# The memory's weights split by adding DMA loads, and S5's sums moved off VectorE and GpSimd, in phase 1 of a streaming encoder step

## The chip, the cores and the metric

The kernel runs on one core of a Trainium2 chip. The time is the device time of one execution in microseconds (us); three executions of the kernel before took 1894.32, 1894.64 and 1896.23 us (median 1894.64). Engines are named as in the profile: PE (TensorE, matrix products; PEld its weight loads), DVE (VectorE), ACT (ScalarE), POOL (GpSimd) and SP (SyncE, which issues most DMAs). Each engine works through its own instructions strictly in order and waits on semaphores for the others.

## The reference, cut to what matters

One inference step of a two-layer encoder, for a prompt of 512 tokens and a running stream of 32, width 1024. Layer 0 mixes tokens with S5, a complex diagonal state-space model in 64 groups of 16 channels with 64 states each; layer 1 uses retention. Each layer then attends to 256 memory tokens and ends in a convolutional feed-forward part.

```python
def s5_discretise(a_re, a_im, log_dt, b_re, b_im, c_re, c_im):
    lam = lax.complex(a_re, a_im)
    dt = jnp.exp(log_dt)[:, None]
    a_bar = jnp.exp(lam * dt)
    b_bar = ((a_bar - 1.0) / lam)[..., None] * lax.complex(b_re, b_im)
...
def s5_block(state, u, a_bar, b_bar, c):
    bu = jnp.einsum('gpc,blgc->blgp', b_bar, u)
    bu = bu.at[:, 0].add(a_bar * state)
    _, xs = lax.associative_scan(_linear_combine, (a, bu), axis=1)
    y = jnp.real(jnp.einsum('gcp,blgp->blgc', c, xs))
...
def memory_kv(mem, g_mem, w_kv):
    m = rms_norm(mem, g_mem) @ w_kv
    k, v = jnp.split(m, 2, axis=-1)
```

All of it is float32. The memory's keys and values of both layers depend on no token, so they can be worked out at any time before the attention of their layer.

## The kernel before, in words

The program runs in stages. Phase 1 computes S5 for all tokens and, in the gaps on PE, the memory's keys and values for both layers. Behind it come the GLU of S5 (its first products are line L233), the attention of layer 0, the feed-forward part, and layer 1.

**Weights in one or two parts.** A float32 product on PE is issued in full (two instructions on PE for one product) or in parts: an operand is rounded to `hi` (type fp32r), `lo` is the rest, and three quick products hi x hi, hi x lo and lo x hi replace the full one (`mm3`, L224 to L226). `weights` loads a tile of 128 x 1024 into one of three raw slots `wr` on SP's queue (L211); `split` rounds it on ACT into one of three slots `wh` (L206) and subtracts on DVE into one of three slots `wl` (L207).

**The memory.** `kv_units` yields the work in units: for each layer an operand step (memory times gain), 8 key tiles and 8 quarters of values, each with one weight tile. `KV_SPLIT = (1,)` names the layers that are worked out in parts: layer 1. Layer 0 takes the raw weights (L492) with full float32 products (L500). The memory's 1 / rms, `mc`, needs square sums (POOL, L447), a small product (L453) and three Newton steps on DVE (`rsqrt_of`, L311 to L315); PE lays it along a row, `mr` (L340), and the keys leave PSUM times `mr` on DVE (L521).

**S5.** Discretisation comes first: `exp_acc`, an exponential by a polynomial on DVE (L620 to L630, twice), sine and cosine on ACT, powers 0 to 8 of the step (`Pr`, `Pi`, by `cmul`, L552 to L557), then `b_bar` (`bb`). The inputs `U` (8 tiles of 128 x 560) need their own 1 / rms, `ur`: ACT squares the eight tiles (L699, L702), POOL adds them up (L703), DVE reduces (L704), PE sums over partitions with the matrix `block` (L707), and DVE takes Newton steps (L709 on). `phases` builds unit phases of a chunk's step to the powers 0 to 64 by squaring (`cmul`) and renormalising (`unit`, L732 to L737), with POOL for half of the wide products. Then, for each eighth e of the groups:

- `matrices` (M): POOL multiplies U by `ur` (L781); DVE makes four products of 128 x 512 in slots of the tags `wh` and `wl` (L789, L790), POOL adds them in pairs (L791), PE turns them (L797) and multiplies with c (L802), ACT copies.
- `states` (S): PE products (L823), four DVE products with the phases (L834 to L838), two POOL sums (L836, L839), two copies (L840, L841), the scans on DVE (L847), and the way back on DVE and POOL (L849 to L860).
- `carry` (C): two DVE products for each half (L873, L875) and their sum on POOL (L877).
- `outputs` (O): PE products (L888, L889), a gelu on ACT (L890), transposes (L898), copies (L900, L901).

The source gives steps in the order of the tables PROLOGUE and ORDER, with the memory's units let in by `fill`; a scheduler then sets the order of instructions on each engine. Slots of a tag are reused in turn, and who reuses one waits until its last reader is done.

Of the kernel before, what the change touches and what calls it, by code (L numbers as in the profile page):

```python
# [13 lines left out]
OP = mybir.AluOpType  # L14
# [38 lines left out]
def constants():  # L53
    """Arrays that depend on shapes alone."""
# [27 lines left out]
def w_tiles(w, mt=None):  # L82
    """[K, M] -> [m tile, 128 of k, K/128 * 128 of m]: one contiguous chunk for an output tile."""
    k, m = w.shape
    a = w.reshape(k // P, P, m // P, P).transpose(2, 1, 0, 3)
    return a.reshape(m // P, P, (k // P) * P)


def layout(inp):
# [29 lines left out]
    cr, ci = f["ssm_c_re"][0], f["ssm_c_im"][0]      # [G, C, 64]  # L119
# [19 lines left out]
    # values: [layer, half of columns, quarter of k, 128, 2 k tiles * 512]  # L139
# [1222 lines left out]
```

## Time and profile before

| | |
|---|---|
| median of three executions | 1894.64 us |
| profiled execution, span from first to last instruction | 1893.0 us |
| PE busy over the span | 1820.2 us (96%) |
| DVE, ACT, POOL busy | 1086.7, 611.6, 384.7 us |
| DMA | 178.02 MB, mean 94 GB/s |
| mean granted PE clock | 0.980 |
| first product of the GLU | at about 248 us |

The profile gives of its own execution the span; what lies around the span is seen against the runs' median. In a row of a timeline stand start, length, engine, line and operation, output and inputs, and the number of instructions merged; in square brackets the idle time of the engine ahead of the row and what ended it. A row of waits has the sum, the number of times and the longest. A group has its count, busy time, mean length in ns, and idle time ahead of it. Where one line has several instructions that overlap, the distance from start to start is the price, not the length.

### The profile page before, as it was taken

Reading aid. Unit: us, or ns where it says so; the run is one execution under the profiler, and the core shown is the slowest. Engines: PE = TensorE matmul, PEld = TensorE weight load, DVE = VectorE, ACT = ScalarE, POOL = GpSimd, SP = SyncE. Lnnn points to the kernel's source line nnn. Section 1 sums busy time; section 2 is a strip of 40 time slices with the busy share of each in tenths; the row PEclk is TensorE's granted clock in tenths of the full one; section 3 lists DMA queues with packets and bytes.
Section 4 is the critical chain, followed back from the end, with each engine's and each line's share of the span. In section 5 each row is a group of like instructions: output and inputs, shape, how many; then the busy total and the mean of one; then the engine's idle time right before and its main releaser. Section 6 shows DMA issues by size and latency. Waiting matters only on the chain.

```text
span 1893.0 us, 32752 instructions
## 1 busy us (share of the span) xinstructions
PE 1820.2 (96%) x13785; PEld 1730.6 (91%) x13785; DVE 1086.7 (57%) x1848; ACT 611.6 (32%) x901; POOL 384.7 (20%) x439
## 2 busy tenths in 40 slices
PE   7868899999999999999999999999999999999998
PEld 6457789999999999999899899998999999999998
DVE  9999856545544535555644646546655554453553
ACT  3132454433323323333223122223444332232333
POOL 7685611011211202121000100100101121120221
PEclk9888989999999999999999999999999999999998
DMA  6434344122222222232222222222411222222221
GB/s 214 132 114 124 120 133 144 68 86 79 90 90 88 78 92 90 72 109 82 76 85 94 79 79 73 90 79 86 138 68 56 87 84 88 90 84 95 90 71 67
DMA packets 65970, 178.02 MB, mean 94 GB/s; under 512 B 8928, under 2 KB 18528, under 8 KB 65824
## 3 DMA queue, kind: packets, MB, share of 16 engines
q1 hardware_dynamic: 65536, 175.79, 27.4%
q8 instruction: 108, 1.77, 0.4%
q14 instruction: 38, 0.31, 0.1%
q10 hardware_dynamic: 288, 0.15, 0.0%
HBM read 162.78 MB, written 10.77 MB: 92 GB/s over the span
## 4 chain that ended last, share of the span: by engine, by line
PE 83%; DVE 2%; issue 1%; ACT 1%; ACTq 0%; DVEq 0%
PE ps L233 74%; PE ps L224 2%; PE ps L225 2%; PE ps L226 2%; PE ps L1286 1%; DVE wl L207 0%; PE ps L1275 0%; PE ps L1248 0%; PE ps L1008 0%; PE ps L1222 0%; ACT wh L206 0%; PE bank L1022 0%; DVE xl L292 0%; PE ps L329 0%; PE ps L403 0%
## 5 line engine op out<-in xcount | busy, mean ns | idle before, releaser
L206 ACT CAST wh<-wr 128x1024 fp32r<-128x1024 f32 (+1 forms) x256 | 264.6, 1037 | 810.2 <-PE ps L233 626.8
L233 PE MATMUL ps<-xh,wh 128*128 128x272 f32 x2432 | 507.5, 290 | 5.4 <-DVE x L356 3.6
L233 PE MATMUL ps<-xl,wh 128*128 128x272 f32 x2432 | 503.6, 288 | 0.0
L233 PE MATMUL ps<-xh,wl 128*128 128x272 f32 x2432 | 502.3, 288 | 0.0
L233 PE MATMUL ps<-r,wh 128*128 128x272 f32 x2688 | 449.2, 289 | 3.0 <-ACT r L901 1.6
L233 PEld LDWEIGHTS ps<-xh,wh 128*128 128x128 f32 x2432 | 380.7, 188 | 11.1 <-ACT r L298 3.7
L233 PEld LDWEIGHTS ps<-r,wh 128*128 128x128 f32 x2688 | 380.2, 189 | 6.4 <-ACT r L206 3.0
L233 PEld LDWEIGHTS ps<-xh,wl 128*128 128x128 f32 x2432 | 382.0, 188 | 2.3 <-issue 2.3
L233 PEld LDWEIGHTS ps<-xl,wh 128*128 128x128 f32 x2432 | 383.0, 189 | 0.3
L207 DVE TENSOR_TENSOR wl<-wr,wh 128x1024 fp32r<-128x1024 f32 (+1 forms) x256 | 321.8, 1260 | 92.3 <-ACT wh L206 84.2
L233 PE MATMUL ps<-r,wl 128*128 128x272 f32 x1344 | 278.0, 288 | 0.0
L233 PEld LDWEIGHTS ps<-r,wl 128*128 128x128 f32 x1344 | 211.2, 189 | 0.0
L356 DVE TENSOR_TENSOR x<-ps,x 128x544 f32<-128x544 f32 x96 | 69.3, 724 | 234.9 <-PE ps L233 234.7
L301 POOL TENSOR_TENSOR acc<-acc,r 128x544 f32<-128x544 f32 x36 | 58.8, 1633 | 453.1 <-ACT r L298 444.6
L1088 POOL COPY nco<-r 128x2 f32<-128x2 f32 x44 | 13.9, 315 | 374.5 <-DVE r L1086 374.5
L1095 DVE TENSOR_TENSOR r<-ps,rr 128x544 f32<-128x544 f32 x44 | 31.9, 725 | 96.7 <-PE ps L233 96.7
L1085 DVE TENSOR_TENSOR r<-ps,rr 128x272 f32<-128x272 f32 x44 | 19.4, 442 | 117.4 <-PE ps L233 117.4
L1146 POOL TENSOR_TENSOR r<-r,r 128x544 f32<-128x544 f32 x8 | 10.8, 1353 | 339.9 <-ACT wh L206 326.0
L1096 POOL TENSOR_TENSOR r<-r,r 128x32 f32<-128x32 f32 x44 | 34.3, 780 | 206.2 <-ACT wh L206 186.2
L206 ACT CAST r<-r 128x544 fp32r<-128x544 f32 x84 | 52.5, 650 | 65.8 <-POOL r L1096 26.2
L1093 DVE SCALAR_TENSOR_TENSOR r<-r,conv,r 128x546 f32<-128x546 f32 x88 | 69.1, 785 | 3.5 <-ACT r L1091 1.9
L207 DVE TENSOR_TENSOR r<-r,r 128x544 fp32r<-128x544 f32 x84 | 59.3, 729 | 14.5 <-ACT r L206 14.3
(354 smaller groups left out, 2109.0 us busy)
## 6 DMA issues: line engine op xcount, KB each, us to landing
wr<-in_w_r SPq DMA_DIRECT2D x48, 512.0 KB, 3.2
wr<-in_w_a SPq DMA_DIRECT2D x44, 512.0 KB, 3.2
wr<-in_w_g SPq DMA_DIRECT2D x44, 512.0 KB, 3.2
wr<-in_w_d SPq DMA_DIRECT2D x32, 448.0 KB, 3.2
wr<-in_w_k SPq DMA_DIRECT2D x16, 512.0 KB, 4.9
wr<-in_w_v SPq DMA_DIRECT2D x16, 512.0 KB, 3.6
wr<-in_w_q SPq DMA_DIRECT2D x16, 512.0 KB, 4.0
wr<-in_w_o SPq DMA_DIRECT2D x16, 512.0 KB, 3.3
```

The lines of the kernel that those rows point to most:

```text
L206: self.nc.scalar.copy(hi, src)
L207: (self.nc.gpsimd if pool else self.nc.vector).tensor_tensor(out=lo, in0=src, in1=hi.bitcast(F32), op=OP.subtract)
L224: mm(out, lhsT=a[0], rhs=b[0], start=start, stop=False)
L225: mm(out, lhsT=a[0], rhs=b[1], start=False, stop=False)
L226: mm(out, lhsT=a[1], rhs=b[0], start=False, stop=stop)
L233: mm(ps[:, h, :TH], lhsT=ws[wi], rhs=x[xi][:, h * TH:(h + 1) * TH], start=start and n == 0, stop=stop and n == 2)
L301: add.tensor_tensor(out=self.acc, in0=self.acc, in1=sq, op=OP.add)
L356: self.nc.vector.tensor_tensor(out=self.halves(x), in0=src, in1=self.halves(x), op=OP.add)
L1085: V.tensor_tensor(out=ext[:, 2:2 + TH], in0=pa[:, 0, :TH], in1=r[:, :TH], op=OP.mult)
L1093: V.scalar_tensor_tensor(out=cv, in0=ext[:, t:t + W], scalar=cw[:, t, f:f + 1], in1=cv, op0=OP.mult, op1=OP.add)
L1095: V.tensor_tensor(out=self.halves(gr), in0=pg[:, :, :TH], in1=self.halves(r), op=OP.mult)
L1096: PL.tensor_tensor(out=gr[:, TP:], in0=gr[:, TP:], in1=cv[:, TP + 2:W], op=OP.mult)
```

## The change

1. `KV_SPLIT = (0, 1)`: layer 0's memory products go in parts too, as layer 1's.
2. A new `weights_loaded` for all 32 tiles of the memory's weights: ACT rounds (`hi`), ACT writes `lo = -hi`, and a DMA on POOL's queue loads the same weights again and adds them to `lo`. No DVE subtraction is left there.
3. `matrices` and `carry`: POOL's sums L791 (16) and L877 (16) become adding DMAs between SBUF tiles, 8 of 128 x 1024 and 16 of 128 x 512.
4. The square sums of U: instead of POOL's seven additions and one small product, PE multiplies every squared tile with `block` in PSUM (16 products of 280 columns), and DVE reduces the result.
5. `exp_acc` joins a product and an addition to one operation; `square` and `unit` work on real and imaginary part together.

Comments are left out in the new file, so its line numbers lie 11 to 13 higher. Cut to its core:

```diff
-KV_SPLIT = (1,)          # layers whose memory projections take operands in two parts
+KV_SPLIT = (0, 1)
...
+    def weights_loaded(self, src):
+
+        raw = self.main.tile([P, 1024], F32, tag="wr", bufs=3, name=self.name("wr"))
+        self.nc.sync.dma_start(out=raw, in_=src)
+        hi = self.main.tile([P, 1024], F32R, tag="wh", bufs=3, name=self.name("wh"))
+        lo = self.main.tile([P, 1024], F32R, tag="wl", bufs=3, name=self.name("wl"))
+        self.nc.scalar.copy(hi, raw)
+        self.nc.scalar.activation(out=lo, in_=hi.bitcast(F32), func=AF.Copy, scale=-1.0)
+        self.nc.gpsimd.dma_start(out=lo, in_=src, accum_op=OP.add)
+        return hi, lo
...
             if l in KV_SPLIT:
-                return self.weights(src)
+                return self.weights_loaded(src)
...
-            V.tensor_scalar(out=p, in0=r, scalar1=1.0 / 5040, scalar2=1.0 / 720, op0=OP.mult, op1=OP.add)
-            for c in (1.0 / 120, 1.0 / 24, 1.0 / 6, 0.5, 1.0, 1.0):
-                V.tensor_tensor(out=p, in0=p, in1=r, op=OP.mult)
-                V.tensor_scalar(out=p, in0=p, scalar1=c, scalar2=None, op0=OP.add)
+            V.tensor_scalar(out=p, in0=r, scalar1=1.0 / 5040, scalar2=None, op0=OP.mult)
+            for c in (1.0 / 720, 1.0 / 120, 1.0 / 24, 1.0 / 6, 0.5, 1.0):
+                V.scalar_tensor_tensor(out=p, in0=p, scalar=c, in1=r, op0=OP.add, op1=OP.mult)
...
-        red, ssum = self.slot(SLOT), st([P, POS], "ssum")
+        ssum = st([P, POS], "ssum")
+        ps = self.bank()
         for e in range(KT):
-            if e == 0:
-                A.activation(out=red, in_=U[e], func=AF.Square)
-            else:
-                sq = self.slot(SLOT)
-                A.activation(out=sq, in_=U[e], func=AF.Square)
-                PL.tensor_tensor(out=red, in0=red, in1=sq, op=OP.add)
-        V.tensor_reduce(out=ssum, in_=red.rearrange("p (g q) -> p q g", g=8), axis=AX.X, op=OP.add)
+            sq = self.slot(SLOT)
+            A.activation(out=sq, in_=U[e], func=AF.Square)
+            for n in range(2):
+                nc.tensor.matmul(ps[:, :4 * POS], lhsT=block, rhs=sq[:, n * 4 * POS:(n + 1) * 4 * POS],
+                                 start=e == 0 and n == 0, stop=e == KT - 1 and n == 1)
+        V.tensor_reduce(out=ssum, in_=ps[:, :4 * POS].rearrange("p (g q) -> p q g", g=4), axis=AX.X, op=OP.add)
...
+        def square(o, a):
+
+            V.tensor_tensor(out=wt, in0=a, in1=a, op=OP.mult)
+            V.tensor_tensor(out=o[:, 0], in0=wt[:, 0], in1=wt[:, 1], op=OP.subtract)
+            V.scalar_tensor_tensor(out=o[:, 1], in0=a[:, 0], scalar=2.0, in1=a[:, 1], op0=OP.mult, op1=OP.mult)
...
             for n in range(2):
                 V.tensor_tensor(out=vb[n], in0=pw[n], in1=bs[n], op=OP.mult)
                 V.tensor_tensor(out=vt[n], in0=pw[2], in1=bs[1 - n], op=OP.mult)
-                PL.tensor_tensor(out=vb[n], in0=vb[n], in1=vt[n], op=OP.add)
+            nc.gpsimd.dma_start(out=vbt, in_=vtt, accum_op=OP.add)
...
-                PL.tensor_tensor(out=y, in0=y, in1=yt, op=OP.add)
+                nc.gpsimd.dma_start(out=y, in_=yt, accum_op=OP.add)
```

The scheduler also moves what stands around these edits. On PE, where the row `mr` of the memory's 1 / rms is laid (L340 before, the operand is `ident` and `mc`), the order before was, with seven key tiles of layer 0 ahead of it (the last in bank_331):

```order
L500 MATMUL bank_331<-r_105,wr_329 128x256 x2
L500 MATMUL bank_331<-r_108,wr_329 128x256 x2
L500 MATMUL bank_331<-r_111,wr_329 128x256
L340 MATMUL bank_241<-ident,mc 128x128 x2
L500 MATMUL bank_331<-r_111,wr_329 128x256
L500 MATMUL bank_346<-r_102,wr_344 128x256 x2
```

It is now, with wh and wl the two parts of a weight tile, bank_131 the first key tile, bank_257 the second and L464 the square sum for `mc`:

```order
L237 MATMUL bank_131<-r_128,wl_99 128x256
L464 MATMUL bank_282<-ones,r_156 128x1 x2
L235 MATMUL bank_307<-r_107,wh_302 128x256
L236 MATMUL bank_307<-r_107,wh_302 128x256
L235 MATMUL bank_340<-r_107,wh_335 128x256
L236 MATMUL bank_340<-r_107,wh_335 128x256
L351 MATMUL bank_282<-ident,mc 128x128 x2
L237 MATMUL bank_257<-r_107,wl_253 128x256
```

One key tile is complete ahead of L351, of three others only the first products with the rounded part stand there.

On POOL, where U is multiplied by `ur` (L781, now L791), the order before was, with the sums of three eighths' matrices (L791) far ahead and the sums of the first states behind:

```order
L791 TENSOR_TENSOR wh_528<-wh_528,wl_529 128x512 x2
L791 TENSOR_TENSOR wh_772<-wh_772,wl_773 128x512 x2
L791 TENSOR_TENSOR wh_949<-wh_949,wl_950 128x512 x2
...
L781 TENSOR_TENSOR u_158<-u_158,ur_463 128x560
...
L781 TENSOR_TENSOR u_165<-u_165,ur_463 128x560
L836 TENSOR_TENSOR r_742<-r_742,r_743 128x280
```

It is now, where L229 is the adding load of a weight tile and L802 the adding transfer of an eighth's matrices:

```order
L229 DMA wl_685<-in_w_v 128x1024
L229 DMA wl_704<-in_w_v 128x1024
L791 TENSOR_TENSOR u_191<-u_191,ur_651 128x560
...
L791 TENSOR_TENSOR u_198<-u_198,ur_651 128x560
L229 DMA wl_731<-in_w_v 128x1024
L802 DMA wh_765<-wl_766 128x1024
L802 DMA wh_967<-wl_968 128x1024
L229 DMA wl_1026<-in_w_v 128x1024
L847 TENSOR_TENSOR r_937<-r_937,r_938 128x280
```

The first two eighths' matrix sums moved from ahead of the eight products to behind them, and twelve adding loads stand ahead of them.

On DVE the Newton steps for `ur` follow the reduction of the square sums (L716); before, they were spread over the phases' operations. They stand now behind the last key tile of layer 0 (bank_497, times `mr`) and ahead of the first matrices' products:

```order
L532 TENSOR_TENSOR rr_486<-bank_461,mr 128x256
L532 TENSOR_TENSOR acc_522<-bank_497,mr 128x256
L716 TENSOR_REDUCE ssum_614<-bank_615 128x70
L719 TENSOR_SCALAR um_649<-ssum_614 128x70
L322 TENSOR_SCALAR ur_651<-um_649 128x70
...
L801 TENSOR_TENSOR wl_766<-PIn_577,bbi_603 128x512
```

The matrices' products of the first three eighths stood ahead of the reduction of the square sums before.

More of the change, by code (lines that the diff above doesn't have):

```diff
@@ L623, in exp_acc @@
             V.scalar_tensor_tensor(out=r, in0=k, scalar=2.12194440e-4, in1=r, op0=OP.mult, op1=OP.add)
-            V.tensor_scalar(out=p, in0=r, scalar1=1.0 / 5040, scalar2=1.0 / 720, op0=OP.mult, op1=OP.add)
-            for c in (1.0 / 120, 1.0 / 24, 1.0 / 6, 0.5, 1.0, 1.0):
-                V.tensor_tensor(out=p, in0=p, in1=r, op=OP.mult)
-                V.tensor_scalar(out=p, in0=p, scalar1=c, scalar2=None, op0=OP.add)
+            V.tensor_scalar(out=p, in0=r, scalar1=1.0 / 5040, scalar2=None, op0=OP.mult)
+            for c in (1.0 / 720, 1.0 / 120, 1.0 / 24, 1.0 / 6, 0.5, 1.0):
+                V.scalar_tensor_tensor(out=p, in0=p, scalar=c, in1=r, op0=OP.add, op1=OP.mult)
             ki = st([P, N], "ki", dt=I32)
             V.tensor_scalar(out=ki, in0=k, scalar1=127.0, scalar2=8388608.0, op0=OP.add, op1=OP.mult)
-            V.tensor_tensor(out=out, in0=p, in1=ki.bitcast(F32), op=OP.mult)
+            V.scalar_tensor_tensor(out=out, in0=p, scalar=1.0, in1=ki.bitcast(F32), op0=OP.add, op1=OP.mult)
         t3 = [sm(f"t{n}") for n in range(3)]
-        dt, zr, zi, rho, cs, sn = (sm(n) for n in ("dt", "zr", "zi", "rho", "cs", "sn"))
+        dt, zr, zi, rho = (sm(n) for n in ("dt", "zr", "zi", "rho"))
+        csn = st([P, 2, N], "csn")
+        cs, sn = csn[:, 0], csn[:, 1]
         exp_acc(dt, ldt, t3)
@@ L694, in phase1 @@
                   [a.rearrange("p (n c) -> p n c", c=C) for a in braw], bt)
-        red, ssum = self.slot(SLOT), st([P, POS], "ssum")
+        ssum = st([P, POS], "ssum")
+        ps = self.bank()
         for e in range(KT):
-            if e == 0:
-                A.activation(out=red, in_=U[e], func=AF.Square)
-            else:
-                sq = self.slot(SLOT)
-                A.activation(out=sq, in_=U[e], func=AF.Square)
-                PL.tensor_tensor(out=red, in0=red, in1=sq, op=OP.add)
-        V.tensor_reduce(out=ssum, in_=red.rearrange("p (g q) -> p q g", g=8), axis=AX.X, op=OP.add)
+            sq = self.slot(SLOT)
[4 more added lines that the diff above has]
+        V.tensor_reduce(out=ssum, in_=ps[:, :4 * POS].rearrange("p (g q) -> p q g", g=4), axis=AX.X, op=OP.add)
         fill(F_NORM)
-        ps = self.bank()
-        nc.tensor.matmul(ps[:, :POS], lhsT=block, rhs=ssum, start=True, stop=True)
         um, ut, ur = st([P, POS], "um"), st([P, POS], "ut"), st([P, POS], "ur")
-        V.tensor_scalar(out=um, in0=ps[:, :POS], scalar1=1.0 / D, scalar2=EPS, op0=OP.mult, op1=OP.add)
+        V.tensor_scalar(out=um, in0=ssum, scalar1=1.0 / D, scalar2=EPS, op0=OP.mult, op1=OP.add)
         self.rsqrt_of(um, ur, ut)
@@ L725, in phase1 @@
         pr, pi = ph[:, 0], ph[:, 1]
-        w1 = [st([P, NP, 1], f"w1{n}") for n in range(2)]
-        w2 = [st([P, NP, 1], f"w2{n}") for n in range(2)]
-        wt = [st([P, NP, 1], f"wt{n}") for n in range(2)]
-        def unit(c):
-            V.tensor_tensor(out=wt[0], in0=c[0], in1=c[0], op=OP.mult)
-            V.tensor_tensor(out=wt[1], in0=c[1], in1=c[1], op=OP.mult)
-            V.tensor_tensor(out=wt[0], in0=wt[0], in1=wt[1], op=OP.add)
-            V.tensor_scalar(out=wt[0], in0=wt[0], scalar1=-0.5, scalar2=1.5, op0=OP.mult, op1=OP.add)
-            for a in c:
-                V.tensor_tensor(out=a, in0=a, in1=wt[0], op=OP.mult)
+        w1, w2, wt = (st([P, 2, NP, 1], f"w{n}") for n in range(3))
+        def square(o, a):
+            V.tensor_tensor(out=wt, in0=a, in1=a, op=OP.mult)
+            V.tensor_tensor(out=o[:, 0], in0=wt[:, 0], in1=wt[:, 1], op=OP.subtract)
+            V.scalar_tensor_tensor(out=o[:, 1], in0=a[:, 0], scalar=2.0, in1=a[:, 1], op0=OP.mult, op1=OP.mult)
+        def unit(c):
+            V.tensor_tensor(out=wt, in0=c, in1=c, op=OP.mult)
+            V.tensor_tensor(out=wt[:, 0], in0=wt[:, 0], in1=wt[:, 1], op=OP.add)
+            V.tensor_scalar(out=wt[:, 0], in0=wt[:, 0], scalar1=-0.5, scalar2=1.5, op0=OP.mult, op1=OP.add)
+            V.tensor_tensor(out=c, in0=c, in1=wt[:, 0:1].to_broadcast([P, 2, NP, 1]), op=OP.mult)
         def phases():
@@ L744, in phases @@
             PL.memset(pi[:, :, 0:1], 0.0)
-            c1 = [a[:, :NP].unsqueeze(2) for a in (cs, sn)]
-            self.cmul(V, w1, c1, c1, wt)
-            self.cmul(V, w2, w1, w1, wt)
-            self.cmul(V, [a[:, :, 1:2] for a in (pr, pi)], w2, w2, wt)
-            unit([a[:, :, 1:2] for a in (pr, pi)])
+            square(w1, csn[:, :, :NP].unsqueeze(3))
+            square(w2, w1)
+            square(ph[:, :, :, 1:2], w2)
+            unit(ph[:, :, :, 1:2])
             s = 2
@@ L752, in phases @@
                 n = min(s, POS - 5 - s)
-                self.cmul(V, [a[:, :, s:s + 1] for a in (pr, pi)], [a[:, :, s // 2:s // 2 + 1] for a in (pr, pi)],
-                          [a[:, :, s // 2:s // 2 + 1] for a in (pr, pi)], wt)
-                unit([a[:, :, s:s + 1] for a in (pr, pi)])
+                square(ph[:, :, :, s:s + 1], ph[:, :, :, s // 2:s // 2 + 1])
+                unit(ph[:, :, :, s:s + 1])
                 if n > 1:
@@ L785, in matrices @@
             pw = [a[:, p0:p0 + 4, :L].unsqueeze(3).to_broadcast(sh) for a in (Pr, PRn, PIn)]
+            vbt, vtt = (self.main.tile([P, 1024], F32, tag=t, bufs=3, name=self.name(t)) for t in ("wh", "wl"))
             vb, vt = ([a[:, n * 512:(n + 1) * 512].rearrange("p (n j c) -> p n j c", n=4, j=L) for n in range(2)]
-                      for a in (self.main.tile([P, 1024], F32, tag=t, bufs=3, name=self.name(t)) for t in ("wh", "wl")))
+                      for a in (vbt, vtt))
             for n in range(2):
```

## The prediction

> **What bounds the kernel now.** I read the page's first part, then three stretches, then the chain of waits.
>
> ```profile
> span 1893.0 us, 32752 instructions
> 0.00:100.00 100.00, 78.78 (x354) 52.96 (x354) 92.65 (x262) 25.11 (x43) 71.31 (x64) 0.91 0.53 180
> 100.00:240.00 140.00, 108.24 (x916) 94.09 (x917) 129.85 (x182) 46.25 (x89) 93.91 (x100) 0.87 0.36 112
> 240.00:1893.00 1653.00, 1633.13 (x12517) 1583.58 (x12515) 864.16 (x1406) 540.19 (x769) 219.50 (x276) 0.99 0.26 87
> 247.86 58.73 PE ps L233 x455
> ```
>
> The columns of a stretch are its length, busy time of PE, PEld, DVE, ACT and POOL, the granted clock, the DMA share and GB/s. From 240 us on PE is 99% busy at clock 0.99; before that DVE is full (93 of 100 and 130 of 140 us) while PE is 77% busy at 0.87 to 0.91. The fifth row, from the chain, is the GLU's start: 1893.0 - 247.9 = 1645.1 us behind it that no edit touches. So the forecast is only when that row comes. The waits of phase 1, and the scans that mark the eighths:
>
> ```profile
> PE bank L340 <- DVE mc L315: 7.1, 1, 7.1
> PE bank L889 <- POOL xl L877: 15.2, 3, 10.2
> DVE r L847 <- POOL r L840: 8.4, 6, 2.4
> 99.94 1.37 DVE L847 TENSOR_TENSOR_SCAN r<-d,r 128x280 f32<-128x280 f32 x2 [1.53 <-POOL r L840]
> 112.78 1.37 DVE L847 TENSOR_TENSOR_SCAN r<-d,r 128x280 f32<-128x280 f32 x2
> 229.86 1.38 DVE L847 TENSOR_TENSOR_SCAN r<-d,r 128x280 f32<-128x280 f32 x2 [1.43 <-POOL r L840]
> ```
>
> That makes 99.9 us to the first scan, 12.8 to the second (which I keep), six even periods of (229.86 - 112.78) / 6 = 19.5 us, and a tail of 18.0 us.
>
> **DVE and POOL, what goes.**
>
> ```profile
> L207 DVE TENSOR_TENSOR wl<-wr,wh 128x1024 fp32r<-128x1024 f32 x18 | 26.5, 1487 | 0.1
> L873 DVE TENSOR_TENSOR xl<-ca,Pr 128x512 f32<-128x512 f32 x12 | 17.8, 1526 | 0.0
> L873 DVE TENSOR_TENSOR xl<-ca,Pr x16: 682/1756/1778, 91.6 to 220.5; 128x512 f32<-128x512 f32 x16
> L877 POOL TENSOR_TENSOR xl<-xl,r 128x512 f32<-128x512 f32 x16 | 26.6, 1680 | 0.0
> L791 POOL TENSOR_TENSOR wh<-wh,wl 128x512 f32<-128x512 f32 x16 | 21.7, 1383 | 18.1 <-DVE wl L790 13.9 <-DVE wh L789 4.2
> L703 POOL TENSOR_TENSOR r<-r,r 128x560 f32<-128x560 f32 x7 | 17.2, 2452 | 0.4
> ```
>
> The sixteen layer-1 subtractions (L207) leave DVE: in an eighth some 2.3 of them, 2.3 x 1.49 = 3.4 us. L873 takes 682 ns at the least and 1526 in the mean while POOL adds (L877); with those sums in DMAs two of them save 2 x 0.85 = 1.7. DVE's period goes from 19.5 to 14.4 us. POOL loses 65.5 us of sums and gains 56 DMA issues (32 loads, 8 for M, 16 for Y). No row has a DMA issued by POOL: between SP's 0.33 us and the 1.7 of the sum replaced, I take 1.2, since POOL's work is slow in all its rows: 67 us, no relief. The joined operations (12 in the two exponentials, about 41 in squares and units) and eight added L476-like operations:
>
> ```profile
> L626 DVE TENSOR_TENSOR t<-t,t 128x96 f32<-128x96 f32 x12 | 4.2, 346 | 0.2
> L554 DVE TENSOR_TENSOR ph<-ph,wt 128x32 f32<-128x32 f32 x7 | 1.5, 208 | 0.0
> L476 DVE SCALAR_TENSOR_TENSOR r<-r,gains,r 128x256 fp32r<-128x256 f32 x8 | 5.7, 773 | 0.0
> 74.01 0.21 DVE L732 TENSOR_TENSOR wt<-ph 128x32 f32<-128x32 f32 x1
> 74.14 0.19 DVE L311 TENSOR_SCALAR ur<-um 128x70 int32<-128x70 int32 x1
> 37.88 1.36 DVE L735 TENSOR_SCALAR wt<-wt 128x32 f32<-128x32 f32 x1
> 41.66 1.88 DVE L789 TENSOR_TENSOR wh<-Pr,bbr 128x512 f32<-128x512 f32 x3
> ```
>
> Small operations start 0.13 apart (74.01, 74.14): 12 x 0.25 + 41 x 0.13 - 8 x 0.77 = 2.1 us less on DVE ahead of the first scan. A small operation that takes 1.36 (37.88) stands behind a POOL sum; some five of these are L703's, 6 us that go. The matrices' first products (from 41.66) now come later.
>
> ACT gains 48 passes of 1.05 us (32 negations, 16 roundings), 50 us on 71 busy of 240: hidden, except in the chain below. SP keeps its 484 rows; a raw slot is free after ACT's rounding, not after DVE's too, which costs nothing.
>
> **PE.**
>
> ```profile
> 7.40 3.67 PE L500 MATMUL bank<-r,wr 128*128 128x256 f32 x16
> 147.20 0.28 PE L225 MATMUL bank<-r,wh 128*128 128x256 f32 x1
> 148.74 0.28 PE L226 MATMUL bank<-r,wl 128*128 128x256 f32 x1
> 118.44 2.13 PE L823 MATMUL bank<-u,xl 128*64 128x70 f32 x32
> 151.28 0.38 PE L889 MATMUL bank<-xl,r 128*69 128x128 f32 x2
> 151.50 0.38 PE L888 MATMUL bank<-M,u 128*69 128x128 f32 x2
> 114.30 1.04 PE L797 MATMUL bank<-ident,wh 128*128 128x128 f32 x8
> 139.67 0.58 PE L226 MATMUL bank<-r,wl 128*128 128x256 f32 x1 [2.46 <-DVE wl L207]
> 144.53 0.41 PE L224 MATMUL bank<-r,wh 128*128 128x256 f32 x1
> ```
>
> A unit of layer 0 in one part costs 3.6 us; in two parts 24 products at (148.74 - 147.20) / 13 = 0.118, so 2.8: 12 us less over sixteen units. Against it stand 32 instructions of L714 on 280 columns, 8 us by L500's 0.23 each. Behind the first scan 19 units are left, 2.4 an eighth (6.7 us); L823 takes 2.1, 16 pairs of products at 0.22 take 3.5, L797 1.0, and I put 1.7 on the other transposes and products of M: 15.0 us at full speed. A wait of 2.46 us shows the slow clock: some 23 products from 139.67 to 144.53 are 0.21 apart, so about 2.3 us are lost. I take one such wait an eighth: 17.3 us.
> By the Trainium skill, "TensorE: Matmul & The Clock Gate", Part 1, the full clock returns after about 3.4 us of steady work, so a wait would lose 1.7 us, the period be 16.7 and the sum 3.6 us lower; the row shows about 5 us at half speed, and the row decides.
>
> **The new waits.** Each load's low part now goes: weights land, ACT rounds, ACT negates, POOL issues, the adding DMA lands, and only then its third product runs.
>
> ```profile
> L206 ACT CAST wh<-wr x19: 1034/1047/1071, 87.3 to 233.6; 128x1024 fp32r<-128x1024 f32 x19
> L492 SPq DMA_DIRECT2D wr<-in_w_v x8: 327/375/403, 35.1 to 79.0; - x8
> DMA to landing us min/median/max: 3.1/3.8/7.1
> L781 POOL TENSOR_TENSOR u<-u,ur 128x560 f32<-128x560 f32 x8 | 12.2, 1566 | 4.2 <-DVE ur L315 4.2
> 44.92 0.23 DVE L315 SCALAR_TENSOR_TENSOR mc<-mt,mc 128x2 f32<-128x2 f32 x1
> 85.30 0.23 DVE L315 SCALAR_TENSOR_TENSOR ur<-ut,ur 128x70 f32<-128x70 f32 x1
> ```
>
> No row has an adding DMA. Below it is bounded by the plain load's 3.1 us, above by twice 7.1, if the target is read as well and the queues are full. Nearest is the median 3.8; with 1.2 of issue and something for the second read I take X = 5.5 us from issue to landing. Three slots (wl) carry the units and the matrices. A unit holds one for 2.1 (ACT twice) + X + about 5 (its products with S5's between) + 3 in queues, my choice; a matrix for 2.5 + X + 1.7 + 3. An eighth's 2.4 units and one matrix then need (2.4 x (10.1 + X) + 7.2 + X) / 3 = 10.5 + 1.13 X = 16.7 us. That is under PE's 17.3, and reaches 19.5 at X = 8. While POOL waits to issue for a unit (for ACT, which waits for PE to free the slot), the products u x ur and the sums of the states stand behind it, and DVE's scan waits for those; on PE a late low part holds up S5's products.
>
> **First piece.** In the new order PE stands at the memory's 1 / rms (L351) after one key tile, not after seven. Its third Newton step ended at 45.2 and now comes about 10 us earlier (2.1, 6 and what L789 took), 35. Six of the seven other tiles and the first values: three at 2.8 us, then six at (2.8 + 2.1 + 5.5) / 3 = 3.5, and some 4 us of L714 that no gap takes: the square sums are whole at 69, ur at 72 (85.5 before). POOL's eight products u x ur take 12.2: 84. Only behind them stand M0's adding DMA and the thirteenth unit's: issued 86, landed about 91, then transposes, copies, first products and sums: first scan near 97, 2.6 us earlier than 99.9. So nearly all of DVE's relief there is lost to the order. Bounds: X from 3.1 to 14 puts it from 8 earlier to 15 later.
>
> **Sum.** First piece -2.6; six periods of 17.3 for 19.5: -13.2; tail +2, since the last Y waits for an issue and a landing instead of two sums of 1.7. In all -13.8: a span of 1879.2. The median of the runs lies 1.6 us above the profiled span (1894.64 against 1893.0), so **1881 us**.
>
> **Rivals.**
> - Relief in full (0.22): PE never waits for a low part, no slow clock: 15.0 us a period, -27, first piece -8, tail +2: 1862. For it: DVE's own need is 14.4, and half the waits above are POOL's or DVE's. Against: in-order queues of four engines now depend on one another.
> - Slots bound (0.23), the other side: X = 10 gives 21.8 us a period, +14; units 5 to 10 of the first piece at 5 us, +9, less the 2.6; the tail +6: 1894.6 + 26 = 1921. It decides from X = 8. For it: the first 100 us already have a DMA share of 0.53, to which 16 more loads come; landing reached 7.1 plain. Against: the share is 0.36 later.
> The Trainium skill, "SBUF — State Buffer" (Who interferes with whom), says that VectorE's two-port operations keep GpSimd from writing descriptors; no run here shows it yet, and it would lengthen X.
> - No change (0.13): the periods drop to 18.5, the first piece comes 4 later by clocks of an idle PE (no products until 35): 1894.6 - 6 + 4 + 2 = 1895.
>
> **Numbers.** Forecast 0.42, taken as 1868 to 1891. The median's 0.2%, about what these runs can tell, is 3.8 us: faster 0.64, same 0.13, slower 0.23. The range, 1850 to 1914, takes in the full relief down to X = 3.1 and the slots up to X = 9; each end leaves about a tenth.
>
> **What would show it.** Right: no DVE subtraction before the GLU, scans 17 us apart, PE idle until about 35 us, ur near 72, the first GLU product near 233. Wrong: POOL DMAs landing after more than 8 us, PE waits on wl in every unit, or the first scan after 105; or the reverse, scans under 15.5 us apart at clock 1.0.

## The result: slower, 1918.4 us for 1894.5

The changed kernel takes 1918.36 us (median of four executions, 1915.95 to 1919.25), the kernel before beside it 1894.48: ratio 1.0125, interval 1.0111 to 1.0139. The forecast was 1881 and faster. The profiled execution has a span of 1917.2 us.

The stretches of the changed kernel (columns as in the prediction: length, PE, PEld, DVE, ACT, POOL, clock, DMA share, GB/s):

```profile
0.00:100.00 100.00, 61.30 (x316) 54.74 (x316) 67.17 (x202) 43.87 (x58) 54.42 (x62) 0.81 0.82 220
100.00:240.00 140.00, 108.12 (x904) 92.85 (x905) 86.62 (x150) 58.31 (x95) 71.55 (x98) 0.86 0.92 213
240.00:272.00 32.00, 26.57 (x206) 21.61 (x205) 19.34 (x31) 17.82 (x29) 15.52 (x20) 1.00 0.99 246
```

DVE is relieved as meant, 86.6 of 140 us where it had 129.9. But PE has 61 of the first 100 us where it had 79, and the DMA share stands at 0.82, 0.92 and 0.99 where it was 0.53 and 0.36: 82 + 129 + 32 = 243 us of all 16 engines, against 103 in 240 before. The scans in DVE's timeline (an eighth has two, here some in one row and some in two):

```profile
114.27 1.35 DVE L858 TENSOR_TENSOR_SCAN r<-d,r 128x280 f32<-128x280 f32 x2
127.60 0.78 DVE L858 TENSOR_TENSOR_SCAN r<-d,r 128x280 f32<-128x280 f32 x1
253.44 0.73 DVE L858 TENSOR_TENSOR_SCAN r<-d,r 128x280 f32<-128x280 f32 x1
```

The first scan is 14.3 us late, the second interval 13.3 us, six periods are (253.44 - 127.60) / 6 = 21.0 us for 19.5, and the tail is 20.5 for 18.0. The DMA queues of the changed kernel within its first 272 us (packets, MB, share of 16 engines), and issues with KB and the median us from issue to landing (the data has arrived):

```profile
q0 software_dynamic: 8064, 25.17, 50.9%
q1 hardware_dynamic: 20974, 34.07, 37.8%
...
wl<-in_w_k POOLq DMA_DIRECT2D x16, 512.0 KB, 8.3
wl<-in_w_v POOLq DMA_DIRECT2D x16, 512.0 KB, 9.5
wh<-wl POOLq DMA_DIRECT2D x8, 512.0 KB, 8.0
```

POOL's adding transfers (q0) move fewer bytes than the plain ones (q1) and take more of the engines: 138 us for 25.17 MB, 182 GB/s, against 331. What PE waits for in phase 1 (us in all, times, longest):

```profile
PE bank L236 <- DMA wl<-in_w_v: 21.3, 9, 6.9
PE bank L237 <- DMA wl<-in_w_k: 19.5, 4, 6.5
PE bank L351 <- DVE mc L326: 10.4, 1, 10.4
```

And the chain of waits, around the first scan and at the GLU's start (start, us, what):

```profile
75.32 6.66 DMA wl<-in_w_v
...
84.41 10.09 POOL u L791 x8
94.50 7.14 DMA wl<-in_w_v
...
101.69 0.79 PE bank L236
...
105.47 0.31 PE bank L236
105.78 0.25 PE bank L237
...
109.37 6.12 DMA wl<-in_w_v
...
273.90 57.13 PE ps L244 x455
```

POOL's products u x ur hold back the issue of a low part, PE stands until that lands at 101.6, runs the unit's products at the slow clock (0.43 us each, until some 105.5), and only then turns M0, whose own transfer had been issued at 96.29. M0's products on DVE had waited for a slot, until PE was done with a unit (in brackets, DVE's idle time):

```profile
90.76 0.96 DVE L801 TENSOR_TENSOR wl<-PIn,bbi 128x512 f32<-128x512 f32 x1 [7.12 <-PE bank L236]
```

From 273.90 on, 1643.3 us are left, as before (1645.1).

### The profile page after: what moved, and what is told of

Read it like the earlier page. It is cut to its first block, busy times and chain, and to the rows that moved or that the text cites. A ratio compares the mean times of both kernels' runs of the same rounds, so it can differ in the third digit from the quotient of the medians.

```text
span 1917.2 us, 33123 instructions
## 1 busy us (share of the span) xinstructions
PE 1821.8 (95%) x13911; PEld 1745.9 (91%) x13911; DVE 1037.2 (54%) x1787; ACT 659.0 (34%) x949; POOL 360.7 (19%) x456
## 3 DMA queue, kind: packets, MB, share of 16 engines
q0 software_dynamic: 8064, 25.17, 7.2%
## 4 chain that ended last, share of the span: by engine, by line
PE 85%; DMA 5%; DVE 3%; issue 2%; POOL 2%; ACT 1%; SPq 1%; POOLq 0%; DVEq 0%; ACTq 0%
PE ps L244 73%; PE ps L235 2%; PE ps L236 2%; PE ps L237 2%; DMA wl<-in_w_v 1%; DMA M<-Fg 1%; DMA wl<-in_w_k 1%; SPq L823 1%; PE bank L236 1%; PE bank L237 1%; PE bank L235 1%; PE ps L1297 1%; POOL u L791 1%; DMA wr<-in_w_k 0%; DVE wl L207 0%
## 5 line engine op out<-in xcount | busy, mean ns | idle before, releaser
L206 ACT CAST wh<-wr 128x1024 fp32r<-128x1024 f32 (+1 forms) x240 | 247.8, 1037 | 763.6 <-PE ps L244 641.6
L207 DVE TENSOR_TENSOR wl<-wr,wh 128x1024 fp32r<-128x1024 f32 (+1 forms) x240 | 296.3, 1238 | 95.8 <-ACT wh L206 87.8
L1096 DVE TENSOR_TENSOR r<-ps,rr 128x272 f32<-128x272 f32 x44 | 19.4, 442 | 117.4 <-PE ps L244 117.4
L1157 POOL TENSOR_TENSOR r<-r,r 128x544 f32<-128x544 f32 x8 | 10.8, 1356 | 339.9 <-ACT wh L206 325.9
```

The source lines that it names most:

```text
L206: self.nc.scalar.copy(hi, src)
L207: (self.nc.gpsimd if pool else self.nc.vector).tensor_tensor(out=lo, in0=src, in1=hi.bitcast(F32), op=OP.subtract)
L1096: V.tensor_tensor(out=ext[:, 2:2 + TH], in0=pa[:, 0, :TH], in1=r[:, :TH], op=OP.mult)
```

## The experiments

All are read by three marks: the first scan, the mean spacing of the eight scans (from the first to the last, over seven), and the first product of the GLU. The marks come from one profiled execution of each kernel, the median from 4 to 10 executions. In every profile 1643 to 1647 us follow the GLU's start, so an execution that lies off its kernel's median shifts the marks with it: the profiled one of e4 is 5.8 us above the median, that of e16 3.7 below, the others are within 2.7. Where marks and medians differ, the medians decide.

| kernel | median us (95% interval of its ratio to the kernel before, run beside it) | first scan | spacing | GLU |
|---|---|---|---|---|
| before | 1894.5 | 99.9 | 18.6 | 247.9 |
| the change | 1918.4 (1.0111 to 1.0139) | 114.3 | 19.9 | 273.9 |
| e1 square sums, joined operations | 1885.7 (0.9954 to 0.9979) | 93.3 | 18.6 | 241.2 |
| e2 = e1 + sums of M, Y by transfers | **1870.7** (0.9872 to 0.9902) | 86.3 | 17.1 | 224.9 |
| e3 = e2 + layer 0 in two parts | 1893.6 (0.9992 to 1.0010) | 107.5 | 17.1 | 247.0 |
| e4 the change, sums by POOL | 1916.8 (1.0116 to 1.0148) | 113.1 | 20.1 | 275.5 |
| e5 the change, half of each adding load | 1904.4 (1.0040 to 1.0070) | 107.3 | 18.9 | 257.9 |
| e6 the change, second loads plain | 1898.8 (1.0019 to 1.0044) | 107.3 | 17.7 | 249.0 |
| e7 the change, layer 0 in one part | 1888.2 (0.9961 to 0.9979) | 85.1 | 19.4 | 239.2 |
| e8 = e2, layer 1 in one part too | 1892.6 (0.9983 to 1.0002) | 102.3 | 17.6 | 245.4 |
| e9 the change, M in general slots | 1981.4 (1.0444 to 1.0472) | 95.4 | 31.4 | 333.2 |
| e10 = e3, M in general slots | 1954.1 (1.0299 to 1.0327) | 100.0 | 26.9 | 306.8 |
| e11 = e2, M in general slots | 1937.0 (1.0200 to 1.0227) | 82.0 | 27.1 | 290.3 |
| e12 the change, two M in general slots | 1917.7 (1.0114 to 1.0141) | 94.7 | 22.3 | 269.0 |
| e13 = e2, two M in general slots | 1871.4 (0.9870 to 0.9903) | 81.6 | 17.6 | 224.0 |
| e14 four slot pairs | 1918.8 (1.0119 to 1.0147) | 103.0 | 21.1 | 270.9 |
| e15 control to e14, three pairs | 1916.7 (1.0101 to 1.0134) | 107.1 | 20.4 | 271.3 |
| e16 = e4, four pairs | 1901.2 (1.0028 to 1.0062) | 103.7 | 18.9 | 251.2 |
| e17 = e5, four pairs | 1909.9 (1.0070 to 1.0100) | 105.3 | 19.4 | 261.2 |
| e18 = e2, Y's sums by POOL | 1876.2 (0.9890 to 0.9918) | 88.3 | 17.9 | 230.6 |

### The change taken apart: e1 to e4

e1: layer 0 in one part, low parts by `split`, both sums on POOL; what stays is the square sums and the joined operations.

```diff
-KV_SPLIT = (0, 1)
+KV_SPLIT = (1,)
-                return self.weights_loaded(src)
+                return self.weights(src)
-            nc.gpsimd.dma_start(out=vbt, in_=vtt, accum_op=OP.add)
+                PL.tensor_tensor(out=vb[n], in0=vb[n], in1=vt[n], op=OP.add)
-                nc.gpsimd.dma_start(out=y, in_=yt, accum_op=OP.add)
+                PL.tensor_tensor(out=y, in0=y, in1=yt, op=OP.add)
```

> Left of the change: the square sums on TensorE and the joined small operations. Layer 0 is back in one part, layer 1's low parts are made by DVE, and the sums of M and Y by POOL. These edits add no transfer. All theories: seven POOL sums of 2.45 us with the DVE waits beside them go (6 us on DVE ahead of the first scan) and 2.1 us of small DVE operations, 32 products of some 8 us come to a PE that is not full there; nothing changes behind the first scan. First scan 94 to 100, period 19.5, time 1889 to 1895. If it is above 1897, the loss of the whole change does not lie with its transfers alone.

e2: the first two of these edits only. e3: the second only (both layers in two parts, DVE's subtraction). e4: the last two only.

> As the harmless kernel, and the sums of M and Y by adding transfers, 24 of them, 8.4 MB; no adding loads, layer 0 in one part. Theory 'bytes' (the 16 DMA engines are full, at some 182 GB/s for an adding transfer): 46 us of DMA time go into phase 1 whose DMA share was 0.43 over 240 us, so there is room, landing stays under 6 us, and DVE and POOL are relieved: 1880 to 1890. Theory 'chain' (an adding transfer is late because of the queues and engines it goes through, whatever the DMA engines do): M's and Y's landing stays near 8 and 6.5 us, each eighth waits for it: 1893 to 1900.

> The whole change, but the low parts of all 32 memory weights are made by DVE's subtraction (1.24 to 1.49 us each) in place of a negation on ACT and an adding load. The 24 adding transfers of M and Y stay. Theory 'bytes': 16.8 of the 25.2 MB of adding transfers go, the DMA share of phase 1 falls from 0.89 to about 0.55, M's landing falls from 8.0 to about 5 us, and DVE becomes the bound again: 32 subtractions in place of 16, 1885 to 1900. Theory 'order' (the memory's 1 / rms comes ahead of the other tiles, and M0 behind u x ur): the first scan stays at 108 or later and the time above 1905. Both leave DVE at over 85% of the stretch 100 to 240.

> The whole change, but the sums of M and Y are made by POOL again; the 32 adding loads stay. Theory 'bytes': the adding transfers fall from 25.2 to 16.8 MB, 138 to 92 us of the 16 engines, the DMA share from 0.89 to about 0.75; landing of the loads falls from 8.4 to 6 or 7 us, and a third to a half of the 24 us is won back: 1904 to 1912. Theory 'chain': the loads' landing and PE's waits for them stay as they are, POOL gets 48 us of sums back with its issues queued behind them: 1916 to 1930.

From row to row of the table, the GLU's start moves by -6.7 (e1), -16.3 (sums by transfers), +22.1 (layer 0 in two parts), +26.9 (adding loads for DVE's subtractions): +26.0 in all. By the medians the last three are -15.0, +22.9 and +24.8. e1 wins a little more than expected, all of it ahead of the first scan. In e2 the transfers have room, and it came 9 us under the range of the theory "bytes":

```profile
0.00:100.00 100.00, 84.41 (x399) 59.66 (x400) 84.09 (x229) 24.69 (x43) 52.90 (x67) 0.94 0.69 211
100.00:240.00 140.00, 118.44 (x1053) 104.66 (x1052) 109.83 (x175) 57.82 (x109) 61.24 (x82) 0.95 0.66 177
```

Those are e2's stretches: PE 84 and 118 us at clock 0.94 and 0.95, DVE at 110, and 0.67 of the DMA engines. The time of e3 fits "bytes", its first scan of 107.5 nearly "order": layer 0's two parts cost 21.2 us ahead of the first scan and nothing in the spacing. The adding loads cost 6.8 ahead of it and 7 x 2.8 = 20 in the spacing. e4 refuted "bytes" in its simple form: 8.4 MB of adding transfers fewer, a DMA share of 0.67 behind 100 us, and landing (8.0 us for 8.4) and time hardly moved, which is what "chain" said. Its queues and landing (first 270 us):

```profile
q1 hardware_dynamic: 20542, 33.02, 37.5%
q0 software_dynamic: 4608, 16.78, 34.1%
...
wl<-in_w_k POOLq DMA_DIRECT2D x16, 512.0 KB, 8.1
wl<-in_w_v POOLq DMA_DIRECT2D x16, 512.0 KB, 8.0
```

### What a load costs: e5 to e8

```diff
-        self.nc.gpsimd.dma_start(out=lo, in_=src, accum_op=OP.add)
+        self.nc.gpsimd.dma_start(out=lo[:, :512], in_=src[:, :512], accum_op=OP.add)   # e5
+        self.nc.gpsimd.dma_start(out=lo, in_=src.bitcast(F32R))                         # e6
```

> The whole change, but each adding load brings only the first 512 of the 1024 columns; the other half of each low part stays minus the rounded weight, so half of the third product's operand is left out (in value, not in work). Same instructions on every engine, same queues and slots; 8.4 MB of adding loads less. Theory 'transfer time' (X, issue to landing, is set by the bytes of the adding transfer): X falls from 8.4 to 5 or 6 us, the slots formula 10.5 + 1.13 X gives 16.7 a period, and the GLU starts 15 to 25 us earlier: 1893 to 1905. Theory 'chain' (X is mostly the queues and the fixed cost of a transfer that POOL issues): X stays at 7 or more, and the time at 1910 to 1918.

> The whole change, but the 32 second loads are plain: POOL issues the same 512 KB into the same tile, and nothing is added, so the low part is the weight itself (the product's value is another one, the work is the same). If the addition is what takes the time: landing 4 to 6 us, its queue's share of the engines falls by some 40 us, and the time is 1893 to 1905. If it is a second load of every weight that does it, or POOL's queue: landing stays at 7 to 8.5 us, 1912 to 1919.

e5 leaves out half of each low part, e6 the subtraction of the rounded weight; PE's products are the same. Landing falls to 6.2 us in both (median of the 32 loads and M's eight transfers; 8.4 in the change), and the medians are 14.0 and 19.6 us lower (the GLU's marks 16 and 25 us earlier). e6 has the same 512 KB and the same queue, so some 20 of the change's 24 us go with the addition, POOL's longer issue (0.86 us for 0.57) included. The queues of e6, and e2's of its 24 adding sums, each in the first 270 us:

```profile
q1 hardware_dynamic: 22473, 37.55, 41.5%
q0 software_dynamic: 8064, 25.17, 36.6%
```

```profile
q0 software_dynamic: 3456, 8.39, 17.5%
```

If the sums take 17.5% in e6 too, that leaves 19.1%, 52 us, for 16.78 MB of plain loads, 325 GB/s. The same bytes with the addition take 34.1% in e4, 92 us, 182 GB/s: 0.56 of the rate. The Trainium skill, "Collectives: The Full Stack", in "The bandwidth ceiling: the fold count and why AG ≠ RS ≠ AR", says of collectives that a reduce-scatter runs at half an all-gather's bandwidth because its addition needs two source reads. The measured 0.56 agrees in size, and no run here separates the second read from the addition.

e7 and e8 change the layers in two parts (`KV_SPLIT = (1,)` in the change, `KV_SPLIT = ()` in e2).

> The whole change with layer 0 in one part: adding loads for layer 1's 16 weights alone. Against the kernel with the same sums and DVE's subtractions, 1870.7. Theory 'slots': periods behind the first scan hold 2 to 2.5 units of layer 1, 10.5 + 1.13 x 8 = 19.5 us against that kernel's 17.9, so 10 us slower than it, with the first scan at 86 to 90 as there: 1878 to 1886. If the loss of the change is mostly layer 0's two parts in the first piece, this kernel is within 5 us of 1870.7, or under it, since DVE is relieved of 24 us.

> The sums of M and Y by adding transfers, square sums and joined operations as in the change, and both layers in one part: no low part is made at all. Layer 1's 16 units cost PE 3.6 us in place of 2.8, 12.8 us in all, and DVE loses 16 subtractions of 1.2 to 1.5 us, 22 us. In the kernel with layer 1 in two parts (1870.7) PE is busy 118 of 140 us and DVE 110. If DVE's and ACT's part of the chain is what sets its periods of 17.9 us, 1860 to 1868; if PE's own work sets them, 1874 to 1884.

In e7 the first scan comes at 85 us again, and sixteen adding loads where e2 subtracts on DVE cost 17.5 us, nearly all in the spacing (7 x 2.35): "slots" nearly, 2 us over its range. e8 missed: 21.9 us slower than e2, and 16 of them lie ahead of the first scan, where neither kernel has come to layer 1 (in e2 its first product runs at 111). Its chain of waits there:

```profile
80.78 8.39 POOL u L791 x7
89.18 5.62 DMA wh<-wl
94.82 1.29 DVE wl L801 x2
97.54 3.44 DVE xl L884 x4
100.98 1.41 DVE wh L800 x2
102.39 1.28 DVE r L858 x2
```

The scheduler has put products of a further matrix and of Y ahead of the first scan (L858) on DVE, and those wait for a slot until M's transfer, behind u x ur on POOL, has landed. So e8 does not tell what layer 1's two parts are worth by themselves.

### Slots or engines: e9 to e17

M's products and sums share the three `wh` and `wl` slots with the units. e9 (on the change), e10 (on e3) and e11 (on e2) take M out:

```diff
-            vbt, vtt = (self.main.tile([P, 1024], F32, tag=t, bufs=3, ...) for t in ("wh", "wl"))
+            vbs, vts = ([self.slot(512) for _ in range(2)] for _ in range(2))
...
-            nc.gpsimd.dma_start(out=vbt, in_=vtt, accum_op=OP.add)
+            for n in range(2):
+                nc.gpsimd.dma_start(out=vbs[n], in_=vts[n], accum_op=OP.add)
```

> The whole change, but the products and sums of M stand in four of the general slots and no longer in the three wh and three wl slots of the weights; M's adding transfer is two of 256 KB in place of one of 512. Same bytes, same engines. Theory 'slots': units alone share the three slots, 2.4 x (10.1 + 8.4) / 3 = 14.8 us an eighth in place of 20, so periods fall to 17 or 18 (DVE, ACT, PE), and M0 can be made while layer 0's units run, so that the first scan comes at 92 to 105 in place of 114: 1875 to 1900. Theory 'bytes' (the 16 DMA engines are full, 0.89 busy): nothing is taken from them, periods stay at 19.5 to 21, the first scan at 110 or later: 1910 to 1920.

> DVE's subtractions for both layers in two parts (1893.6 us, first scan at 107.5), with M's products and sums out of the weights' slots. Theory 'slots': of the 21 us by which the first scan comes later with layer 0 in two parts than in one (107.5 against 86.3), most is M0 waiting for a wh and a wl slot behind all units of the first piece; it falls to 90 to 98, the time to 1878 to 1888. Theory 'DVE full' (16 more subtractions of some 1.3 us, 21 us, stand on an engine that is 90% busy in the first 100 us): the first scan stays at 103 or later, the time at 1888 or above.

> The best kernel so far (sums of M and Y by adding transfers, layer 0 in one part, DVE's subtractions, 1870.7) with M out of the weights' slots. There the first three M are made at 31 to 40 us, while the slots stand empty, so the first scan stays at 84 to 88. Behind it an eighth holds 2.4 units of layer 1 and one matrix; with subtractions by DVE a slot is held some 8 us, (2.4 x 10 + 8) / 3 = 10.7 us, far under the period of 17.1, so both theories give 0 to 5 us less: 1865 to 1872. A larger gain would say that slots bound even this kernel.

The first scans came earlier, by 18.9 us in the change as "slots" said, by 7.5 in e3 (100.0, between its two theories; that DVE's subtractions hold the rest is not shown), and by 4.3 in e2, 2 us more than expected there. But all three lost 60 to 66 us in all, which no theory had. DVE's timeline of e11, with idle time in brackets:

```profile
135.28 0.68 DVE L799 TENSOR_TENSOR r<-Pr,bbr 128x512 f32<-128x512 f32 x1
...
137.09 0.68 DVE L800 TENSOR_TENSOR r<-PIn,bbr 128x512 f32<-128x512 f32 x1
...
151.44 0.29 DVE L820 TENSOR_TENSOR Fg<-bank,Fg 128x128 f32<-128x128 f32 x1 [11.01 <-PE bank L816]
```

A matrix is now made just ahead of its use (products to 137.8, its M part at 151.4), with DVE idle for 11 us while transfer, transposes and products run; in e2 the products stand an eighth ahead. So the spacing of these three says nothing on whether slots or engines bind. e12 and e13 move only the first two matrices (`if e < 2`), on the change and on e2:

> The whole change, but the first two matrices' products and sums stand in general slots, the other six in the weights' as before. Theory 'slots' for the first piece: the first scan comes at 95 to 100 as in the run with all eight moved, the periods stay at 20, so the GLU starts 14 to 19 us earlier: 1898 to 1906. If the shorter first piece is given back later (DMA engines full), the time stays above 1912.

> The best kernel so far (1870.7: sums of M and Y by adding transfers, layer 0 in one part, low parts by DVE) with its first two matrices in general slots. With all eight moved its first scan came at 82.0 in place of 86.3, so up to 4 us may be won if the general slots hold out behind it: 1866 to 1871. If two matrices are enough to crowd the general slots, 1872 to 1885.

e12 shows it plainly:

```profile
94.70 1.37 DVE L866 TENSOR_TENSOR_SCAN r<-d,r 128x280 f32<-128x280 f32 x2 [1.73 <-POOL r L859]
...
250.99 0.73 DVE L866 TENSOR_TENSOR_SCAN r<-d,r 128x280 f32<-128x280 f32 x1
```

The first scan is 19.6 us earlier, the last only 2.5, and the time is the same (1917.7): what the first piece won is given back behind it, at a DMA share of 0.91 and 0.88. e13 equals e2 in time, and there too an earlier first scan (4.7 us) is given back, by a second scan 20.1 us later instead of 12.4, though the DMA share behind 100 us is only 0.66:

```profile
81.61 1.37 DVE L866 TENSOR_TENSOR_SCAN r<-d,r 128x280 f32<-128x280 f32 x2 [0.80 <-POOL r L859]
101.67 1.37 DVE L866 TENSOR_TENSOR_SCAN r<-d,r 128x280 f32<-128x280 f32 x2 [1.40 <-POOL r L859]
```

So an earlier first scan that wins nothing does not by itself show that the DMA engines are full.

e14 gives the memory's weights a fourth pair of slots (every fourth weight; M has two tiles, the raw weights two slots, to make room); e15 is its control without the fourth pair; e16 and e17 are e4 and e5 with the fourth pair.

```diff
+        self.nw = getattr(self, "nw", 0) + 1
+        pool, n = (self.sp, 1) if self.nw % 4 == 0 else (self.main, 3)
+        hi = pool.tile([P, 1024], F32R, tag="wh", bufs=n, name=self.name("wh"))
+        lo = pool.tile([P, 1024], F32R, tag="wl", bufs=n, name=self.name("wl"))
```

> The whole change with a fourth pair of slots, used by every fourth weight of the memory; to make room, M has two tiles in place of three and the raw weights two slots in place of three, as in the control. The GLU's part behind phase 1 is slower by the missing raw slot, so only the row of the GLU's start is read. Theory 'slots': an eighth needs (2.4 x 18.5 + 15.4) / 4 = 15 us of four slots in place of 20 of three, so periods fall to 17 or 18 and the GLU starts 12 to 20 us earlier than in the control. Theory 'bytes': within 4 us of the control.

> The control: the whole change with two tiles of M and two raw slots, and three pairs of slots for the weights. If M's and the raw slots do not matter in phase 1, the first scan at 112 to 116, periods of 20 us, the GLU's start at 272 to 277; the time longer than 1918 by what the missing raw slot costs behind it.

> The kernel with a fourth pair of slots (two tiles of M, two raw slots), with M's and Y's sums by POOL: DMA share about 0.62 to 0.7 behind the first scan. Read against the GLU's start of 275.5 us with POOL's sums and three slots. If two limits stand side by side (the DMA engines with all adding transfers, the slots without M's and Y's), the GLU starts 10 to 20 us earlier here: 255 to 265. If POOL's queue binds (issues behind sums), within 4 us of 275.

> The fourth pair of slots, and adding loads that bring only half of the columns (the other half of each low part stays minus the rounded weight: left out in value, not in work). Read against the GLU's start of 257.9 us with half loads and three slots. If slots bind once the engines have room, 240 to 252; if the transfers' time still binds (share 0.82 to 0.92 there), within 4 us of 258.

By the medians the fourth pair wins nothing with all adding transfers (1918.8 us against e15's 1916.7), 15.6 us with POOL's sums (1901.2 against e4's 1916.8; the marks say 24.3, but e4's are those of its longest execution and e16's those of its shortest), and with half loads it loses 5.5 (1909.9 against e5's 1904.4; 3.2 by the mark, within the 4 given for "the transfers' time still binds"). In e14 landing is 9.1 us in the median, and ACT, which stood for slots, now stands for the raw weights:

```profile
0.00:100.00 100.00, 69.14 (x442) 60.16 (x442) 71.80 (x212) 51.55 (x70) 51.35 (x66) 0.85 0.90 244
100.00:240.00 140.00, 101.89 (x835) 87.94 (x835) 82.79 (x151) 58.98 (x96) 70.80 (x102) 0.87 0.92 215
```

```profile
ACT wh L229 <- DMA wr<-in_w_v: 32.1, 7, 12.0
```

What is shown is a pair of limits. With M's and Y's sums as transfers a fourth pair of slots moves nothing (e14); with three pairs, taking these sums back to POOL moves nothing (e4); both together win: e16 is 17.6 us faster than e14, which differs from it in these sums alone. One limit is the three slots, held for a landing of 8.0 us in e4. What the other is stays open. The engines' time fits e14 (share 0.92 behind 100 us) and e16 (0.74). But e17 has e16's share over 240 us (0.80 for 0.79) and 96 us of adding transfers for 92, and its fourth pair wins nothing. It keeps M's and Y's transfers, and PE waits for Y's, where in e16 it waits little for POOL's sums (first 280 us):

```profile
PE bank L902 <- DMA xl<-r: 23.6, 8, 12.6
PE bank L902 <- POOL xl L890: 5.0, 2, 4.2
```

So the landing of these transfers can be the second limit as well. And in e14 ACT stood 48 us for raw weights, in e15 2 us: a fourth pair with three raw slots was not run. One reserve more: what makes room for the fourth pair was controlled with the sums as transfers only. e15's GLU starts 2.6 us earlier than the change's and its first scan comes at 107.1, ahead of the 112 to 116 expected, so the room is not quite neutral; with POOL's sums it was not run.

### Which sum: e18

e2 with Y's sums on POOL.

> The best kernel (1870.7) with Y's sums by POOL again, and only M's by adding transfers. POOL gets 16 sums of 1.7 us back, 3.4 an eighth, and DVE's products beside them take 1.53 for 0.77 us, 1.5 an eighth more; PE's waits for Y's landing (15.4 us in six) go. If relief of DVE is what won 15 us, half to all of it is lost: 1878 to 1886. If it was M's sums, off the path from DVE's products to the transposes, 1868 to 1874.

5.5 us slower than e2, between the two expectations: M's sums by transfer give about 9.5 of e2's 15 us over e1, Y's the rest, although PE waits 15.4 us for Y's landing in e2 (six waits). **e2 is the best kernel found**: 1870.7 us, 0.9887 of before.

## Why the prediction was wrong

**Phase 1 alone: right.** 1643.3 us behind the GLU's start, and all 26 us ahead of it.

**DVE's relief and the sums: right where they stand alone, and worth more than thought.** The products beside the sums (changed kernel, groups by line up to 272 us: busy, mean ns) took 1.53 us before:

```profile
L884 DVE TENSOR_TENSOR xl<-ca,Pr 128x512 f32<-128x512 f32 x16 | 11.6, 767 | 0.0
```

By themselves the square sums, joined operations and sums by transfers start the GLU 23 us earlier (e2). An issue by POOL, taken as 1.2 us, took 0.86.

**The failed step: "X = 5.5".** It was sized between plain landings, 3.1 to 7.1 us. It measured 8.4 (median of the loads and M's transfers; 4.9 at the least, 11.8 at the most; 8.8 for the 32 loads alone), past the 8 from which the rival "slots bound" decides. By the prediction's own formula 10.5 + 1.13 x 8.4 = 20.0 us an eighth; the six periods are 21.0, where PE's 17.3 was forecast. The span came 38.0 us over the forecast's 1879.2: 22.0 in the six periods, 17.0 in the first piece. And where X fell to 6.2, for which the formula gives 17.5, the spacing fell to 17.7 (e6) and 18.9 (e5). Of the signs that were to show it wrong two came, landing over 8 us and a first scan after 105; PE waited for a low part 13 times in 32 units, not in every one.

What lengthened X is argued only in part. The rival's "against" (a share of 0.36 later on) took the share of the kernel before for room, without putting 25 MB to it: they need 138 us, on 103 in 240. Even at the plain rate the forecast's phase of 234 us would have had to hold 103 + 77; at the adding rate it is 241, more than there is. But X does not follow the engines' share alone: from 100 to 240 us the adding loads of e4 land in 7.6 us (median) at a share of 0.67, the plain ones of e6 in 6.3 at 0.88. Between these two X goes with the addition.

So the rival's time came (1921, against 1918.4), in part by luck: it put 14 us into the periods, where 9 came, and 6 into the first piece, where 14 came. Its slots are half of the cause: a fourth pair wins only where M's and Y's sums are no transfers (e14, e16), and what holds the time otherwise stays open.

**"A unit in two parts saves 12 us on PE": the wrong term for the first piece.** PE was not what set it (61 us busy of the first 100). With layer 0 in two parts, DVE's subtractions or the adding loads stand ahead of every unit, and the units fill the slots in which the first three matrices were made at 31 to 38 us in e2; in the change M0's products waited until 90.8. Layer 0 in two parts puts the first scan 21 us later with DVE's subtractions (e2 to e3) and 29 with adding loads (e7 to the change). With M in slots of its own the first scan comes 18.9 us earlier in the change (e9) and 7.5 in e3 (e10), so M's wait for a slot is much of the first and less of the second.

**First piece, by its steps (forecast: measured).** The norm at 35: 38. Square sums at 69: PE's last at 80. ur at 72: 83.6. u x ur 12.2: 10.8 us. M0 issued at 86: 96.3. First scan at 97: 114.3, since M0's transposes stood behind a unit whose low part POOL had issued only after u x ur. The coupling was named, X made it long. But 11 of the 17 us were lost by the square sums already: by the forecast's own term, (2.8 + 2.1 + 8.4) / 3 = 4.4 us for 3.5, the six units there cost some 5.8 more, and the norm came 3 later.

**Clock and tail.** "One wait an eighth" was too few: the clock is 0.86 behind 100 us, 0.87 before. After a wait the changed kernel's products stay at the slow spacing for 3.8 us in the chain above (0.43 us each, 101.7 to 105.5) and for 5.9 behind a wait of 5.4 us (0.21 us each, which take 0.12 at full speed); the granted clock is 0.50 in both:

```profile
55.05 0.58 PE L237 MATMUL bank<-r,wl 128*128 128x256 f32 x1 [5.45 <-DMA wl<-in_w_k]
...
60.98 0.35 PE L237 MATMUL bank<-r,wl 128*128 128x256 f32 x1
```

The Trainium skill's "TensorE: Matmul & The Clock Gate", Part 1, gives some 3.4 us of steady work until the full clock. Both stretches are longer, and the forecast's 5 lies between them. The tail is 2.5 us longer, as taken (2).

**VectorE's locks.** The Trainium skill's "SBUF — State Buffer", Who interferes with whom, says that VectorE's two-port operations starve GpSimd of the port time for writing descriptors, which would lengthen X. POOL's issues take 0.86 us in the median and 1.54 at the most, so at the issue it is 0.7 us at the most; what lies between issue and landing no run splits by this cause.

## What to carry to other kernels

Add up the DMA engines' time, not the bytes: here an adding transfer took 1.8 times a plain one's for the same bytes. And look at how long a buffer is held until the transfer into it lands: with a landing of 8.4 us for the 5.5 assumed, an eighth took 21.0 us for the 17.3 forecast. Moving a cheap subtraction (1.2 to 1.5 us on DVE) into a second load of 512 KB was a bad trade here (24.8 us lost by the medians, e3 to the change), moving small sums of data that is in SBUF already a good one (15.0 us won, e1 to e2), while the engines had room. When a single lever does nothing (e4, e14), try the pair before calling the cause refuted. And when marks are read from one profiled execution, hold them against the medians: e4 and e16 differ by 24 us in the first and by 16 in the second.

## What was not expected of the hardware

An adding load of 512 KB took 5.2 us from issue to landing at the least (e4) and 8.0 to 8.8 in the median (e4, the change), a plain one from the same queue 3.9 and 6.0 (e6). M's adding transfer, between SBUF tiles, took 4.7 at the least and 6.0 in the median where no adding loads ran (e3). POOL's issue of an adding load takes 0.86 us, of a plain one 0.57. And the rate of 182 GB/s for additions was the same with 16.8 MB (e4) and with 25.2 MB (the change) in the phase.
